# One group of V products per unit instead of two, with the softmax sums in its bank and the maxima turned by DMA

## The chip, the cores and the metric

The kernel runs on one core of a Trainium2 chip. The metric is the device time of one launch in microseconds; three runs are given as a median. Beside the runs stands one execution that the hardware profiler recorded.

## The reference

One encoder block is applied with shared weights to two requests of 2048 tokens (s = 0, 1). The part that matters here is the grouped-query attention: 8 query heads, 2 key/value heads of 64 channels, blocks of 128 queries.

```python
def one_block(qblk):
    s = jnp.einsum('bkgqd,bskd->bkgqs', qblk, k).astype(jnp.float32) * scale
    pr = jax.nn.softmax(s, axis=-1).astype(v.dtype)
    return jnp.einsum('bkgqs,bskd->bqkgd', pr, v)
...
a = _blocked_gqa(q, k, v) * jax.nn.silu(ga)
fo = _fourier_branch(f, w_fmix) * jax.nn.silu(gf)
h = h + jnp.concatenate([a, fo], axis=-1) @ w_out
gate = jax.nn.sigmoid(_rmsnorm(h, g_ple) @ w_ple_gate)
return h + (p @ w_ple) * gate
```

A block is 128 queries; those of a group's four heads (g) meet the 2048 keys of their key/value head (k). All inputs and outputs are float32.

## The kernel before

The program has three stages. First the input projection is computed for all tokens (line 451). Then attention runs, with the rest of the block, called filler here, between its pieces: the Fourier branch first (lines 1018, 1066, 1030), then the output projection and the gates token tile by token tile (lines 451, 1484, 1375 to 1538). What of the filler is left runs after attention.

Attention goes through 64 units `u`, each one request, one key/value head and one block of 128 queries, so four heads at once: 512 columns, head by head. A unit has eight steps `j`, one for each 256 keys. The loop at the end of `attention` counts steps as `g`, with u = g // 8 and j = g % 8. One step does this:

- `flush` runs what earlier steps deferred (divisions, stores).
- `scores`: TensorE multiplies queries and keys in fp16, in two row halves of 64 (shape 64*128, line 1147), into two PSUM banks. In step 0 a product of `kone` with `mr` first puts the negated row maxima there. ScalarE makes the exponentials `p` (line 1150), of fp32, one buffer `p32` a step. GpSimd adds them up over the steps into `acc` (lines 1153 and 1155) and after step 7 adds the two halves of `acc` (line 1157).
- `lead` runs 14 steps ahead: the score products for the maxima of a later unit (line 1174, into the only `ps_m` buffer) and their reduction on VectorE (line 1182). `negate` writes the negated maxima into `nm` in step 3 of the unit before.
- In step 4, `max_rows` turns `nm` with a TensorE product against the identity (line 1197, shape 128*128) and VectorE spreads it over the heads into `mr` (line 1199). `sums` makes the column sums of the unit before with a product of `acc` and ones (line 1243, shape 128*64), in the same bank, and `divide` takes their reciprocal there (line 1250) and multiplies (line 1251).
- In steps 0 and 4, after the rest, `pv` multiplies the exponentials of four steps with V in fp32 (line 1211, shape 128*64). Even and odd key chunks go to the two column halves, so that both halves of the result hold partial sums over keys of all four heads. `gather` adds them: ScalarE copies the crossed quarters (line 1227) and VectorE adds (line 1233).

After each step the loop yields a share, and `interleave` takes filler worth that share of the time that is left to spread. A step with `pv` yields 0. Filler is taken in whole slots. Every engine and the DMA queue of SyncE run their instructions one after the other: TensorE, ScalarE, VectorE and SyncE in the order in which the program writes them; GpSimd's order during attention is set by a scheduler.

Of the kernel before, what the change touches and what calls it, by code (L numbers as in the profile page):

```python
# [10 lines left out]
F32 = mybir.dt.float32  # L11
# [21 lines left out]
PVG = 4  # L33
# [7 lines left out]
P32 = 7  # L41
# [99 lines left out]
class Build:  # L141
# [963 lines left out]
    def attention(self, kvp):  # L1105
# [84 lines left out]
        def negate(u):  # L1190
            m = M4.pop(u)
            nc.scalar.activation(nm[:].rearrange("p (e c) -> p e c", e=2)[:, :, 0:4],
                                 m[:].unsqueeze(1).to_broadcast([128, 2, 4]), AF.Copy, scale=-1.0 / K_ONE)

        def max_rows(u, ps):

            nc.tensor.matmul(ps, nm[:], id16[:], start=True, stop=True)
            MR[u] = mr = kvp.tile([128, 4, 128], F16, name="mr", bufs=1)
            return lambda: nc.vector.tensor_tensor(out=mr[:], in0=ps.unsqueeze(1).to_broadcast([128, 4, 128]),
                                                   in1=own[:].unsqueeze(2).to_broadcast([128, 4, 128]), op=ALU.mult)  # L1200

        def pv(u, j0):
# [3 lines left out]
            o = O[u]  # L1206
            for j in range(j0, j0 + PVG):
                p = P.pop((u, j))
                for e in range(2):
                    c = 2 * j + e  # L1210
                    nc.tensor.matmul(o[64 * e:64 * e + 64, :], vt[s, kv, c // 8][:, c % 8, :], p[:, e, :],  # L1211
                                     start=(j == 0), stop=(j == 7))
            if j0 + PVG == 8:
# [3 lines left out]
                gather(u)  # L1217

        def gather(u):

            o = O.pop(u)
            tb = pool.tile([128, 2, 128], F32, name="tb", bufs=1)
            at = pool.tile([128, 2, 128], F32, name="at", bufs=2)
            AT[u] = at
            ov = o[:].rearrange("p (c e q) -> p e c q", e=2, q=128)
            for e in range(2):
                nc.scalar.activation(tb[64 * e:64 * e + 64], ov[64 - 64 * e:128 - 64 * e, e], AF.Copy,  # L1227
                                     scale=self.sc["a_scale"][64 - 64 * e:128 - 64 * e, :])

            def add():  # L1230
                for e in range(2):
                    sl = slice(64 * e, 64 * e + 64)
                    nc.vector.scalar_tensor_tensor(out=at[sl], in0=ov[sl, e], scalar=self.sc["a_scale"][sl, :],
                                                   in1=tb[sl], op0=ALU.mult, op1=ALU.add)

            self.defer(lambda: self.defer(add))

        def sums(u, ps):

            acc = ACC.pop(u)  # L1240
# [625 lines left out]
```

## Time and profile before

| | us |
|---|---|
| median of 3 runs (lowest, highest) | 2710.22 (2709.16, 2711.73) |
| span of the profiled execution | 2706.9 |
| median less that span | 3.3 |
| TensorE busy in it | 2623.5 |
| GpSimd busy in it | 1638.0 |
| VectorE busy in it | 1701.7 |
| ScalarE busy in it | 1215.2 |

The profiled execution has no time of its own beyond its span; the 3.3 us are what the runs have around it. In the profile PE is TensorE's matmuls, PEld its weight loads, DVE VectorE, ACT ScalarE, POOL GpSimd, SP SyncE. A shape such as 128*64 is the rows and columns of the array that an instruction uses. A matmul's duration includes its way through the array, and matmuls follow each other faster than that, so starts are compared.

### The profile page before, as it was taken

What the parts mean: (1) busy time and instruction counts of PE and PEld (TensorE: products, weight loads), DVE (VectorE), ACT (ScalarE), POOL (GpSimd) and SP (SyncE); (2) the same over time, 40 slices, a digit from 0 to 9 for tenths busy, and PEclk for the clock granted to TensorE, in tenths of its full rate; (3) what the DMA queues carried; (4) which work ended last, traced back from release to release, by engine and by line L of the source; (5) the groups of instructions that cost most, each with busy time, mean ns of one, the idle gap of its engine ahead of it and who ended that gap; (6) DMA issues with size and microseconds to landing.
All of it is one profiled execution on the core that took longest, in us unless ns stands there. A gap on an engine that the chain in (4) does not pass through costs nothing.

```text
span 2706.9 us, 46069 instructions
## 1 busy us (share of the span) xinstructions
PE 2623.5 (97%) x18112; PEld 1257.0 (46%) x18112; DVE 1701.7 (63%) x2478; ACT 1215.2 (45%) x2047; POOL 1638.0 (61%) x1395
## 2 busy tenths in 40 slices
PE   6899999999998998999999999999999999999998
PEld 3465565655555553444444444344444334444443
DVE  6756465565555785666676767665666666667634
ACT  4543243343224553554544555545545454454442
POOL 1233233242335896787777877777777777777760
PEclk9999999999999999999999999999999999999999
DMA  7467676586527663122222223322232222222222
GB/s 236 134 180 193 175 205 180 157 194 145 150 67 226 212 223 95 48 63 62 75 64 59 58 67 82 96 57 69 57 84 56 66 71 67 59 75 72 59 72 72
DMA packets 418553, 296.71 MB, mean 110 GB/s; under 512 B 259456, under 2 KB 360000, under 8 KB 418336
## 3 DMA queue, kind: packets, MB, share of 16 engines
q1 hardware_dynamic: 405424, 252.01, 35.4%
q0 software_dynamic: 12912, 41.77, 4.2%
q8 instruction: 141, 2.31, 0.3%
q14 instruction: 76, 0.62, 0.1%
HBM read 149.50 MB, written 86.51 MB: 87 GB/s over the span
## 4 chain that ended last, share of the span: by engine, by line
PE 89%; DVE 5%; issue 2%; ACT 1%; DMA 1%; POOL 0%; SPq 0%; DVEq 0%; ACTq 0%; POOLq 0%
PE ps_g L1484 22%; PE ps_x L451 17%; PE ps_o L1211 16%; PE ps_s L1147 13%; PE ps_f L451 7%; PE ps_g L451 7%; PE ps_m L1174 4%; PE ps_f L1243 1%; DVE a_mx L1182 1%; PE ps_g L1018 1%; PE ps_x L917 1%; DVE h L1524 1%; DVE w_mx L312 1%; PE ps_g L1066 0%; PE ps_f L1066 0%
## 5 line engine op out<-in xcount | busy, mean ns | idle before, releaser
L1155 POOL TENSOR_TENSOR acc<-acc,p 128x1024 f32<-128x1024 f32 x384 | 919.5, 2395 | 213.0 <-ACT p L1150 177.0
L1150 ACT ACTIVATE p<-ps_s,s_scale 128x512 f32<-128x512 f32 x1024 | 648.2, 684 | 649.7 <-PE ps_s L1147 624.9
L1182 DVE TENSOR_REDUCE a_mx<-ps_m 128x1 f32<-128x1024 f32 x498 | 609.1, 1223 | 521.3 <-PE ps_m L1174 513.7
L1484 PE MATMUL ps_g<-w_pg,hT 64*128 64x512 f16 x2784 | 493.9, 377 | 5.7 <-DMA hT<-h_hl 5.2
L1211 PE MATMUL ps_o<-p,v 128*64 128x512 f32 x2048 | 464.8, 596 | 0.0
L451 PEld LDWEIGHTS <-uc 128*128 128x128 f16 x3072 | 301.4, 98 | 311.4 <-issue 23.3
L1147 PE MATMUL ps_s<-q,k 64*128 64x512 f16 x3072 | 436.5, 378 | 5.2 <-ACT p L1150 5.2
L1484 PEld LDWEIGHTS <-hT 64*128 64x128 f16 x2784 | 205.2, 94 | 167.0 <-issue 21.4
L1147 PEld LDWEIGHTS <-k 64*128 64x128 f16 x3072 | 151.7, 94 | 249.5 <-issue 127.5
L1484 PE MATMUL ps_g<-w_wo,mh 64*128 64x512 f16 x1440 | 260.8, 377 | 2.8 <-DVE mh L1394 1.6
L1211 PEld LDWEIGHTS ps_o<-p,v 128*64 128x64 f32 x2048 | 141.4, 137 | 255.9 <-issue 246.7
L1484 PE MATMUL ps_g<-w_wo,mT 64*128 64x512 f16 x1440 | 257.7, 376 | 0.0
L1174 PE MATMUL ps_m<-k,q 64*128 64x512 f16 x996 | 202.9, 378 | 16.8 <-DVE a_mx L1182 12.5
L1153 POOL TENSOR_TENSOR acc<-p,p 128x1024 f32<-128x1024 f32 x64 | 150.8, 2356 | 72.8 <-ACT p L1150 72.2
L451 PEld LDWEIGHTS <-w_ga 128*128 128x128 f16 x1536 | 150.0, 99 | 47.2 <-issue 18.2
L934 POOL DMA_DIRECT2D gfd<-gt x32 | 19.6, 614 | 226.7 <-DVE gt L962 192.1
L1484 PEld LDWEIGHTS <-mh 64*128 64x128 f16 x1440 | 101.1, 94 | 91.8 <-issue 16.7
L1484 PEld LDWEIGHTS <-mT 64*128 64x128 f16 x1440 | 102.4, 94 | 83.6 <-issue 4.0
L1227 ACT ACTIVATE tb<-ps_o,a_scale 64x256 f32<-64x256 f32 x128 | 60.1, 469 | 165.8 <-PE ps_o L1211 165.0
L1250 DVE RECIPROCAL ps_f<-ps_f 128x256 f32<-128x256 f32 x59 | 103.6, 1756 | 16.3 <-PE ps_f L1243 16.3
L451 PE MATMUL ps_x<-uc,w_ga 128*128 128x256 f16 x960 | 108.1, 273 | 0.0
L952 POOL DMA_DIRECT2D agd<-gat x64 | 35.3, 553 | 118.4 <-DVE gat L962 113.2
(330 smaller groups left out, 3382.0 us busy)
## 6 DMA issues: line engine op xcount, KB each, us to landing
q<-qTd SPq DMA_DIRECT2D x256, 64.0 KB, 2.2
ag<-agd SPq DMA_DIRECT2D x64, 256.0 KB, 3.3
out<-h POOLq DMA_DIRECT2D x31, 512.0 KB, 3.0
x<-in_x_prompt SPq DMA_DIRECT2D x16, 512.0 KB, 4.7
gfd<-gt POOLq DMA_DIRECT2D x32, 256.0 KB, 2.6
gd<-ge POOLq DMA_DIRECT2D x32, 256.0 KB, 3.1
agd<-gat POOLq DMA_DIRECT2D x64, 128.0 KB, 2.7
w_st<-in_w_out SPq DMA_DIRECT2D x32, 256.0 KB, 3.8
```

What stands on the lines that cost most here:

```text
L451: self.nc.tensor.matmul(ps, lhs(ia, k), rhs(ib, k), start=(i == 0), stop=(i == 3 * ks - 1))
L952: nc.gpsimd.dma_start(self.agd[s][1, r * 128:(r + 1) * 128, c * n:(c + 1) * n], gt[:, :n])
L1147: nc.tensor.matmul(S[u][e][:], w[sl], q[sl].rearrange("p h q -> p (h q)"), start=j == i == 0, stop=i + 1 == len(todo), skip_group_check=True)
L1150: nc.scalar.activation(p[:, e, :], S[u][e][:], AF.Exp, scale=self.sc["s_scale"][:])
L1153: nc.gpsimd.tensor_tensor(out=ACC[u][:], in0=P[u, 0][:], in1=p[:], op=ALU.add)
L1155: nc.gpsimd.tensor_tensor(out=ACC[u][:], in0=ACC[u][:], in1=p[:], op=ALU.add)
L1174: nc.tensor.matmul(ps[c], Q[u][0][sl, h, :], kt[s, kv, half][sl, :, 0, :], start=True, stop=True)
L1182: nc.vector.reduce_max(MX[u][:, h, half, c:c + 1], x, axis=AX.X)
L1211: nc.tensor.matmul(o[64 * e:64 * e + 64, :], vt[s, kv, c // 8][:, c % 8, :], p[:, e, :], start=(j == 0), stop=(j == 7))
L1227: nc.scalar.activation(tb[64 * e:64 * e + 64], ov[64 - 64 * e:128 - 64 * e, e], AF.Copy, scale=self.sc["a_scale"][64 - 64 * e:128 - 64 * e ...
L1250: nc.vector.reciprocal(r, r)
L1484: nc.tensor.matmul(g[0][:], g[1](ia, k)[sl], g[2](ib, k)[sl], start=a, stop=z, skip_group_check=True)
```

## The change

`PVG` goes from 4 to 8: the products with V of a whole unit stand in one group, in step 0 of the next unit, and step 4 has none. The column halves no longer hold even and odd key chunks but two heads each: every chunk of V is loaded for both halves and multiplied with 256 columns in each, over all keys, so `gather` is not needed any more. The sums follow at once in the same group, into columns 256 to 511 of the same bank, and the division is deferred by one step: a reciprocal from PSUM to SBUF and one multiplication with the scale. The maxima are turned by a DMA transpose that SyncE issues in step 4; `nm` is four times as wide for it, and `mr` is written by the DMA. `p32` has ten buffers instead of seven, and the space for descriptors of GpSimd's DMAs is 4096 bytes a partition instead of 16384. Filler now has seven steps of a unit instead of six, by the expression with `PVG` in `run`, and deferred slow work runs three at a time after a group.

```diff
-PVG = 4
+PVG = 8
...
-P32 = 7
+P32 = 10
...
         def negate(u):
             m = M4.pop(u)
-            nc.scalar.activation(nm[:].rearrange("p (e c) -> p e c", e=2)[:, :, 0:4],
+            nc.scalar.activation(nm[:].rearrange("p h (e c) -> p e h c", e=2)[:, :, :, 0],
                                  m[:].unsqueeze(1).to_broadcast([128, 2, 4]), AF.Copy, scale=-1.0 / K_ONE)
 
-        def max_rows(u, ps):
-
-            nc.tensor.matmul(ps, nm[:], id16[:], start=True, stop=True)
+        def max_rows(u):
+
             MR[u] = mr = kvp.tile([128, 4, 128], F16, name="mr", bufs=1)
-            return lambda: nc.vector.tensor_tensor(out=mr[:], in0=ps.unsqueeze(1).to_broadcast([128, 4, 128]),
-                                                   in1=own[:].unsqueeze(2).to_broadcast([128, 4, 128]), op=ALU.mult)
+            nc.sync.dma_start_transpose(mr[:], nm[:].rearrange("p h c -> p (h c)"))
 
         def pv(u, j0):
...
-            o = O[u]
+            o, r = O[u][:, 0:256], O[u][:, 256:512]
             for j in range(j0, j0 + PVG):
-                p = P.pop((u, j))
+                p = P.pop((u, j))[:].rearrange("p e (c f q) -> p e f c q", f=2, q=128)
                 for e in range(2):
                     c = 2 * j + e
-                    nc.tensor.matmul(o[64 * e:64 * e + 64, :], vt[s, kv, c // 8][:, c % 8, :], p[:, e, :],
-                                     start=(j == 0), stop=(j == 7))
+                    for f in range(2):
+                        nc.tensor.matmul(o[64 * f:64 * f + 64], vt[s, kv, c // 8][:, c % 8, :], p[:, e, f],
+                                         start=(c == 0), stop=(c == 15))
...
-                gather(u)
-
-        def gather(u):
...
-        def sums(u, ps):
...
+                av = ACC.pop(u)[:, 0, :].rearrange("p (c f q) -> p f c q", f=2, q=128)
+                for f in range(2):
+                    nc.tensor.matmul(r[64 * f:64 * f + 64], self.ones[:], av[:, f], start=True, stop=True)
+                self.defer(lambda: divide(u))
+
+        def divide(u):
+
+            s, kv, t = units[u]
+            at = pool.tile([128, 2, 128], F32, name="at", bufs=2)
             o = O.pop(u)
...
-            nc.vector.reciprocal(r, r)
-            nc.vector.tensor_tensor(out=x, in0=x, in1=r, op=ALU.mult)
+            nc.vector.reciprocal(x, o[:, 256:512])
+            nc.vector.scalar_tensor_tensor(out=x, in0=o[:, 0:256], scalar=self.sc["a_scale"][:], in1=x,
+                                           op0=ALU.mult, op1=ALU.mult)
...
             if j == 4:
-                ps = self.bank()
                 if u + 1 < n:
-                    turned = max_rows(u + 1, ps[:, 256:384])
-                if u > 0:
-                    sums(u - 1, ps[:, 0:256])
-                    divide(u - 1, ps[:, 0:256])
-                if u + 1 < n:
-                    turned()
+                    max_rows(u + 1)
             heavy = (g - 1) % PVG == PVG - 1 and 0 <= g - 1 < 8 * n
             if heavy:
-                self.run_slow(1 if j else 2)
+                self.run_slow(3)
                 pv((g - 1) // 8, (g - 1) % 8 - PVG + 1)
...
-    nc = bacc.Bacc("TRN2", target_bir_lowering=False, num_devices=1)
+    nc = bacc.Bacc("TRN2", target_bir_lowering=False, num_devices=1, dynamic_dma_scratch_size=4096)
```

In the changed kernel the lines shift: the products with V are L1210, the sums L1218, the transpose L1198, the division L1227 and L1228, and what was L1375, L1484 and L1526 is L1343, L1452 and L1494.

TensorE before, in step 4 of a unit around 1500 us: the maxima of a later unit, the turning of `nm`, the sums of the unit before, four steps' products with V, and the next step's scores (a row x2 is one product for each column half).

```order
L1174 MATMUL ps_m<-k_7155,q_15561 128x512
L1197 LDWEIGHTS nm
L1197 MATMUL ps_f<-id_7187,nm 128x128
L1243 MATMUL ps_f<-acc,ones 64x256 x2
L1211 MATMUL ps_o<-p_15567,v_7161 64x512 x2
L1211 MATMUL ps_o<-p_15600,v_7161 64x512 x2
L1211 MATMUL ps_o<-p_15637,v_7161 64x512 x2
L1211 MATMUL ps_o<-p_15672,v_7161 64x512 x2
L1147 LDWEIGHTS k_7158
```

TensorE after, in step 0 of the next unit at about the same place: the maxima, the one group with eight steps' products and the sums, and then filler.

```order
L1174 MATMUL ps_m<-k_7171,q_15434 128x512
L1210 MATMUL ps_o<-p_15440,v_7177 64x256 x4
L1210 MATMUL ps_o<-p_15495,v_7177 64x256 x4
L1210 MATMUL ps_o<-p_15535,v_7177 64x256 x4
L1210 MATMUL ps_o<-p_15563,v_7177 64x256 x4
L1210 MATMUL ps_o<-p_15624,v_7179 64x256 x4
L1210 MATMUL ps_o<-p_15658,v_7179 64x256 x4
L1210 MATMUL ps_o<-p_15692,v_7179 64x256 x4
L1210 MATMUL ps_o<-p_15708,v_7179 64x256 x4
L1218 MATMUL ps_o<-acc,ones 64x256 x2
L1452 LDWEIGHTS mh
```

The product with `nm` is gone from TensorE, the sums moved from step 4 to the end of step 0, behind L1210, and step 4's maxima are followed by filler.

GpSimd before, in the 50th unit: its seven additions, the addition of the two halves, and a filler addition L1375 that needs loaded data.

```order
L1153 TENSOR_TENSOR acc<-p_23038,p_23113 128x1024
L1155 TENSOR_TENSOR acc<-acc,p_23150 128x1024
L1155 TENSOR_TENSOR acc<-acc,p_23185 128x1024
L1155 TENSOR_TENSOR acc<-acc,p_23221 128x1024
L1155 TENSOR_TENSOR acc<-acc,p_23253 128x1024
L1375 TENSOR_TENSOR ag<-ag 128x512
L1155 TENSOR_TENSOR acc<-acc,p_23293 128x1024
L1155 TENSOR_TENSOR acc<-acc,p_23328 128x1024
L1157 TENSOR_TENSOR acc<-acc 128x512
L1526 DMA out<-h 128x1024
```

GpSimd after, in the same unit:

```order
L1153 TENSOR_TENSOR acc<-p_23503,p_23560 128x1024
L1343 TENSOR_TENSOR ag<-ag 128x512
L1155 TENSOR_TENSOR acc<-acc,p_23596 128x1024
L1155 TENSOR_TENSOR acc<-acc,p_23634 128x1024
L1155 TENSOR_TENSOR acc<-acc,p_23671 128x1024
L1155 TENSOR_TENSOR acc<-acc,p_23700 128x1024
L1155 TENSOR_TENSOR acc<-acc,p_23740 128x1024
L1155 TENSOR_TENSOR acc<-acc,p_23768 128x1024
L1157 TENSOR_TENSOR acc<-acc 128x512
L1494 DMA out<-h 128x1024
```

The filler addition moved from behind the fifth addition to behind the first.

VectorE after, at a unit's edge (before, the division stood in step 4 as L1250, L1251 and L1199):

```order
L1362 SCALAR_TENSOR_TENSOR mh<-ag,mix_s,mh 128x1024
L1227 RECIPROCAL at<-ps_o 128x256
L1228 SCALAR_TENSOR_TENSOR at<-ps_o,a_scale,at 128x256
L1182 TENSOR_REDUCE a_mx<-ps_m 128x1
L1187 TENSOR_REDUCE a_m_14922<-a_mx 128x4
```

The division stands directly ahead of step 1's reduction of maxima (L1182), which completes a unit's maxima (L1187).

More of the change, by code (lines that the diff above doesn't have):

```diff
@@ L1216, in pv @@
                         del vt[s, kv, b]
-                gather(u)
-        def gather(u):
-            o = O.pop(u)
[L1222 to L1236, printed above, removed]
-        def sums(u, ps):
-            acc = ACC.pop(u)
-            av = acc[:, 0, :].rearrange("p (c e q) -> p e c q", e=2, q=128)
-            for e in range(2):
-                nc.tensor.matmul(ps[64 * e:64 * e + 64], self.ones[:], av[:, e], start=True, stop=True)
-        def divide(u, r):
-            s, kv, t = units[u]
-            at = AT.pop(u)
+                av = ACC.pop(u)[:, 0, :].rearrange("p (c f q) -> p f c q", f=2, q=128)
[5 more added lines that the diff above has]
+            at = pool.tile([128, 2, 128], F32, name="at", bufs=2)
+            o = O.pop(u)
             x = at[:].rearrange("p c q -> p (c q)")
-            nc.vector.reciprocal(r, r)
-            nc.vector.tensor_tensor(out=x, in0=x, in1=r, op=ALU.mult)
+            nc.vector.reciprocal(x, o[:, 256:512])
+            nc.vector.scalar_tensor_tensor(out=x, in0=o[:, 0:256], scalar=self.sc["a_scale"][:], in1=x,
+                                           op0=ALU.mult, op1=ALU.mult)
             def store():
@@ L1262, in attention @@
             load_q(kv)
-        id16 = kvp.tile([128, 128], F16, name="id16", bufs=1)
-        nc.gpsimd.tensor_copy(id16[:], self.ident[:])
-        nm = kvp.tile([128, 128], F16, name="nm", bufs=1)
+        nm = kvp.tile([128, 4, 128], F16, name="nm", bufs=1)
         nc.gpsimd.memset(nm[:], 0.0)
@@ L1268, in attention @@
         nc.gpsimd.memset(kone[:], K_ONE)
-        own = kvp.tile([128, 4], F32, name="own", bufs=1)
-        nc.gpsimd.tensor_tensor(out=own[:], in0=self.ident[:, 0:4], in1=self.ident[:, 64:68], op=ALU.add)
         def lead(g):
@@ L1284, in leads @@
                 if g == -2:
-                    max_rows(0, self.bank()[:, 0:128])()
+                    max_rows(0)
         self.ahead = leads()
```

## Prediction

> **What bounds the kernel now.** I read the page's totals first, then the chain that ended last, then busy time by stage.
>
> ```profile
> span 2706.9 us, 46069 instructions
> PE 2623.5 (97%) x18112; PEld 1257.0 (46%) x18112; DVE 1701.7 (63%) x2478; ACT 1215.2 (45%) x2047; POOL 1638.0 (61%) x1395
> PE 89%; DVE 5%; issue 2%; ACT 1%; DMA 1%; POOL 0%; SPq 0%; DVEq 0%; ACTq 0%; POOLq 0%
> ...
> 871.00:1011.00 140.00, 135.77 (x962) 78.07 (x963) 107.94 (x143) 82.89 (x137) 123.96 (x72) 1.00 0.68 216
> ...
> 1100.00:1700.00 600.00, 592.96 (x4414) 249.36 (x4412) 406.66 (x422) 305.00 (x509) 462.34 (x370) 1.00 0.25 66
> ...
> 2300.00:2628.00 328.00, 327.36 (x2469) 137.79 (x2467) 200.17 (x203) 163.14 (x270) 247.72 (x213) 1.00 0.24 66
> ```
>
> The columns of a stretch are PE, PEld, DVE, ACT, POOL, granted clock, DMA share. In the two long stretches PE is busy all but 1% of the time at full clock, and the chain is 89% PE. So a microsecond taken from PE's stream is a microsecond of the kernel, and work taken from DVE or ACT is worth nothing by itself. POOL is the second engine to watch: 77% in the long stretch (462.34 of 600), 89% in the Fourier stretch (123.96 of 140). The sum is made against this execution's 2706.9 us span; the median of the runs is 2710.22, 3.3 us above it, and I carry those 3.3 us over unchanged. What this kernel's measurement can tell from no change is about 0.2%, 5.4 us.
>
> **PE, the term that pays.** The two groups of one unit, the one of step 4 and the one of step 0, as PE ran them:
>
> ```profile
> 1496.47 0.40 PE L1174 MATMUL ps_m<-k,q 64*128 64x512 f16 x2
> 1496.80 0.23 PE L1197 MATMUL ps_f<-id,nm 128*128 128x128 f16 x1
> 1496.96 0.65 PE L1243 MATMUL ps_f<-acc,ones 128*64 128x256 f32 x4
> 1497.44 3.60 PE L1211 MATMUL ps_o<-p,v 128*64 128x512 f32 x16
> 1500.98 0.82 PE L1147 MATMUL ps_s<-q,k 64*128 64x512 f16 x6
> ...
> 1509.06 0.39 PE L1147 MATMUL ps_s<-mr,kone 64*128 64x512 f16 x2
> 1509.28 0.81 PE L1147 MATMUL ps_s<-q,k 64*128 64x512 f16 x6
> 1509.93 0.38 PE L1174 MATMUL ps_m<-k,q 64*128 64x512 f16 x2
> 1510.24 3.65 PE L1211 MATMUL ps_o<-p,v 128*64 128x512 f32 x16
> 1513.83 0.82 PE L1147 MATMUL ps_s<-q,k 64*128 64x512 f16 x6
> 1514.48 0.38 PE L1174 MATMUL ps_m<-k,q 64*128 64x512 f16 x2
> 1514.70 0.38 PE L1484 MATMUL ps_g<-w_wo,mh 64*128 64x512 f16 x1
> ```
>
> Starts are what counts, since ends overlap. The weight loads beside the first group give the rhythm inside it:
>
> ```profile
> 1496.96 0.20 PEld L1243 LDWEIGHTS ps_f<-acc,ones 128*64 128x64 f32 x4
> 1497.23 0.36 PEld L1211 LDWEIGHTS ps_o<-p,v 128*64 128x64 f32 x4
> 1497.88 0.14 PEld L1211 LDWEIGHTS ps_o<-p,v 128*64 128x64 f32 x2 [0.29 <-issue]
> 1498.30 0.14 PEld L1211 LDWEIGHTS ps_o<-p,v 128*64 128x64 f32 x2 [0.29 <-issue]
> 1498.73 0.14 PEld L1211 LDWEIGHTS ps_o<-p,v 128*64 128x64 f32 x2 [0.29 <-issue]
> ```
>
> Each fp32 product shows as two instructions, one pass each, and the two column halves run side by side. A pair of 512-column passes takes 0.43 us (1498.30 to 1498.73), and eight of them make 3.43 us.
>
> Step 4 costs 1500.98 - 1496.47 = 4.51 us from the maxima to the next scores; step 0 costs 1513.83 - 1509.93 = 3.90 us. An ordinary step goes from its maxima to the next work in 0.22 us (1514.48 to 1514.70). So one visit to this shape costs 3.90 - 3.43 - 0.22 = 0.25 us beyond its columns, and step 4, with a third shape ahead of it for L1197, costs 4.51 - 3.43 - 0.22 - 0.43 = 0.43 us beyond its columns and the sums'.
>
> The changed unit has one visit: 32 pair-passes of 256 columns for V, then two for the sums. What does such a pass cost? Below stands half of 0.43, 0.215 us; above stands the sums group as it is, 1496.96 to 1497.44, 0.48 us for two, or 0.24 us each. The second number holds the exposed first load of a visit (step 0's first pass starts at 1510.24 and the group needs 0.05 us more than step 4's for the same columns: 1513.83 - 1510.24 is 3.59 against 1500.98 - 1497.44 = 3.54). Without those 0.05 the two take 0.43, so I use 0.216. The ends of the bound are 34 x 0.215 = 7.31 and 34 x 0.24 = 8.16 us.
>
> After: 0.25 + 34 x 0.216 + 0.22 = 7.81 us, and step 4 becomes ordinary, 0.22. Saved: 4.51 + 3.90 - 7.81 - 0.22 = 0.38 us a unit, 64 units, **24.3 us**. With 0.24 a pass it would be a loss of 0.44 us a unit, 28 us. Filler now stands in seven steps instead of six; counting shape changes in the new order, it enters and leaves its 128x128 shape 13 times more, at about 0.1 us each: **1.3 us** back. PE's net is **-23.0 us**.
>
> By the Trainium skill's TensorEngine Tiling (Array Packing), Instruction Overhead, a matmul has about 60 cycles of overhead; as an addition to each of the 16 extra pair-passes that is an estimated 25 ns each, 26 us in all, and the gain is gone. By its TensorE: Matmul & The Clock Gate, Part 3, a weight load overlaps a matmul in flight only where the row group differs. Both halves use all rows here, so by it the 16 extra loads of 0.14 us would show, 2.2 us a unit; the trace disagrees, since 0.14 us loads already fit inside a 0.43 us rhythm of bare columns.
>
> **POOL, the term that takes.** The sums need the last addition of L1157. Today PE asks for it four steps into the next unit; now at the end of step 0's group. Two units, POOL at their edge; the next unit's first scores start at 1509.06 and 2229.55:
>
> ```profile
> 1502.96 9.66 POOL L1155 TENSOR_TENSOR acc<-acc,p 128x1024 f32<-128x1024 f32 x4
> 1512.70 2.13 POOL L1157 TENSOR_TENSOR acc<-acc 128x512 f32<-128x512 f32 x1
> ...
> 2229.55 0.39 PE L1147 MATMUL ps_s<-mr,kone 64*128 64x512 f16 x2
> ...
> 2229.60 1.27 POOL L1375 TENSOR_TENSOR ag<-ag 128x512 f32<-128x512 f32 x1 [4.15 <-DVE a_mx L1182]
> 2230.83 5.67 POOL L1155 TENSOR_TENSOR acc<-acc,p 128x1024 f32<-128x1024 f32 x2
> 2236.57 2.12 POOL L1157 TENSOR_TENSOR acc<-acc 128x512 f32<-128x512 f32 x1
> ```
>
> The new sums would start 1510.24 - 1509.06 + 0.05 + 32 x 0.216 = 8.1 us after those scores. In the first unit POOL is done 5.8 us after them, 2.3 us early; in the second 9.1 us after, 1.0 us late. Everything PE has queued stands behind that wait. How often?
>
> ```profile
> L1155 POOL TENSOR_TENSOR acc<-acc,p 128x1024 f32<-128x1024 f32 x384 | 919.5, 2395 | 213.0 <-ACT p L1150 177.0
> L1153 POOL TENSOR_TENSOR acc<-p,p 128x1024 f32<-128x1024 f32 x64 | 150.8, 2356 | 72.8 <-ACT p L1150 72.2
> L1157 POOL TENSOR_TENSOR acc<-acc 128x512 f32<-128x512 f32 x64 | 94.4, 1475 | 4.9
> POOL ag L1375 <- DMA ag<-agd: 54.7, 23, 7.2
> PE ps_m L1174 <- DVE a_mx L1182: 12.5, 15, 1.7
> L1150 ACT ACTIVATE p<-ps_s,s_scale 128x512 f32<-128x512 f32 x1024 | 648.2, 684 | 649.7 <-PE ps_s L1147 624.9
> L1251 DVE TENSOR_TENSOR at<-at,ps_f 128x256 f32<-128x256 f32 x59 | 24.8, 421 | 2.0
> L1227 ACT ACTIVATE tb<-ps_o,a_scale 64x256 f32<-64x256 f32 x128 | 60.1, 469 | 165.8 <-PE ps_o L1211 165.0
> L1250 DVE RECIPROCAL ps_f<-ps_f 128x256 f32<-128x256 f32 x59 | 103.6, 1756 | 16.3 <-PE ps_f L1243 16.3
> DMA to landing us min/median/max: 3.0/3.1/5.8
> ```
>
> (The last row is of hT's 64 transposes.) The additions are (919.5 + 150.8 + 94.4) / 64 = 18.2 us a unit. A unit now takes (2229.55 - 1509.06) / 26 = 27.7 us, 26 units lying between those two scores; in the Fourier stretch five units take the 140 us, 28.0 each. So with filler POOL works 0.771 x 27.7 = 21.3 us a unit in the long stretch and 0.885 x 28.0 = 24.8 in the Fourier stretch. After the change it gets its first addition only when the group's sums (0.43), step 1's scores (0.65), two exponentials (1.37) and, by estimate, 1 us of filler are through, 3.5 us, so it has 27.7 - 0.4 - 3.5 = 23.8 us before the next sums, or 24.1. In the long stretch 2.5 us are to spare on average; in the Fourier stretch 0.7 are missing in each of five units, which with its unevenness I take for **6 us**. In the long stretch POOL stands 23 times at L1375 for a landing, 2.4 us on average, just what is spare. The new order puts L1375 earlier in its unit, which helps, but seven additions now follow each other with no PE group among them, so that less is caught up. I take half of those 23 units as late by 1 us: **11 us**. The bounds are nothing, as the first unit shows, and the second unit's 1.0 us in each of 57 units with the 6 before, 63 us; I stay near the first end, since the averages leave time.
>
> **The other edits.** The division (1.76 us and, like L1251, 0.42) now stands on DVE ahead of step 1's maximum, and PE's next maxima wait for that reduction. From the sums' end that is 2.2 us of division and, like any reduction, about 1.2 us, 3.4 us, against two score groups, one maxima and two filler slots on PE, about 1.5 + 2.6. It is hidden where the slots are full, and DVE loses L1199, the multiply and two half-height passes in exchange; L1174 waits 12.5 us in all now. I take **0**, with bounds of -5 and +10. ACT loses L1227, 60 us of work that nothing on the chain waits for: 0. The transpose of the maxima is issued at step 4, behind `negate` of step 3, and is needed four steps, some 10 us, later; landing takes 3.1, at most 5.8 us. SP stands there until ACT has written `nm`, and what queues behind are loads and stores of later steps: 0, bounds 0 and 5. The store of `at` leaves three steps earlier than now, which nobody waits for. Ten buffers hold a unit's eight and two more, so no exponential waits for the later release: 0. For POOL's smaller descriptor space no row shows a wait: 0, bounds 0 and 5.
>
> **Sum.** -23.0 + 6 + 11 = -6 us. Some of PE's small waits of today, the 12.5 us at L1174 among them, will fall together with waits for POOL, worth by estimate another 2 us: 2706.9 - 8 = 2699 of span, and with the 3.3 us outside it **2702 us**.
>
> **Rivals.** With W for PE's waits at the sums, the time is 2710.2 - 25 + W; my forecast is W from 10 to 20, its own range 2695 to 2705.
> - POOL is in time nearly everywhere, W under 10, about 5: 2690. For it: L1375 moves earlier. Against: the second unit above. Chance 0.17.
> - POOL takes the whole gain, W from 20 to 30: 2710, no change. For it: 0.8 us in each of some 30 units is enough. Against: 2.5 us spare on average. Chance 0.24.
> - Slower by POOL: PE stands at L1218 for L1157 by more than 0.48 us a unit on average, W over 30, the point from which it decides. At 0.75 us, W is 48: 2733. For it: POOL's additions are pressed together at 77% load, and the second unit is late already. Against: the first is 2.3 us early. Chance 0.19.
> - A 256-column pass costs the upper 0.24 us: 28 us lost instead of 24.3 gained, with the same waits 2754. Against: the 0.05 us of the first load explain that bound. Chance 0.02.
> - Weight loads show, 16 more a unit at 0.14 us: 64 x 2.24 = 143 us more, 2845. Against: the rhythm above. Chance 0.02.
> - The transposed maxima come late to each unit's first scores, by 1 us: 2702 + 64 = 2766; it would take landings beyond 10 us. Chance 0.01.
>
> **Numbers.** The forecast has chance 0.35. Faster by over 0.2% (under 2704.8) is it and the first rival, 0.52; within 0.2% is the second, 0.24; slower is the rest, 0.24. The range is 2687 to 2728: the low end is PE's net without a wait, the high end holds about half of the slower rival and leaves out some 0.15 above.
>
> **What would show it.** L1210's weight loads should start 0.216 us apart, and one unit should show one L1210 group of about 7 us. L1218 should wait for POOL's last addition, 6 us in total before 1011 us and some 11 later; under 5 or over 25 in total decides between the rivals. L1174's waits should stay near 12 us, and the first scores should never wait for `mr`. A rhythm above 0.22 us, or a wait ahead of the step-1 maxima, would make the prediction wrong.

## The result and the profile after

The changed kernel is slower: 2771.8 us (median of four runs, 2769.4 to 2779.2) against 2711.0 us for the kernel before in the same job, a ratio of 1.0228 with an interval of 1.0213 to 1.0243. That is 61 us more, where 8 us less was forecast; the rival that named PE standing at the sums for POOL had been given 2733 us.

From the page of the changed kernel, its span, busy times and chain:

```profile
span 2767.6 us, 49738 instructions
...
PE 2634.8 (95%) x20096; PEld 1428.1 (52%) x20096; DVE 1648.8 (60%) x2286; ACT 1153.6 (42%) x1919; POOL 1660.6 (60%) x1393
...
PE 67%; POOL 16%; DVE 7%; issue 4%; DMA 3%; ACT 3%; SPq 1%; POOLq 0%; DVEq 0%; ACTq 0%
```

Two of the stretches shown of before, with the same columns (PE, PEld, DVE, ACT, POOL, granted clock, DMA share):

```profile
871.00:1011.00 140.00, 136.46 (x1106) 91.64 (x1104) 97.45 (x126) 78.14 (x126) 122.55 (x71) 0.99 0.76 231
1100.00:1700.00 600.00, 568.59 (x4838) 289.66 (x4836) 366.28 (x337) 267.59 (x438) 448.07 (x344) 0.99 0.27 65
```

PE's share of the chain fell from 89% to 67%, POOL's rose from 0 to 16%, DVE's from 5 to 7%. In the stretch from 1100 to 1700 us PE has holes of 31 us where it had 7. The Fourier stretch, where I had seen POOL fullest, is nearly as before.

Two successive units on PE, the first in time, the second not:

```profile
1332.70 0.40 PE L1174 MATMUL ps_m<-k,q 64*128 64x512 f16 x2
1333.02 7.13 PE L1210 MATMUL ps_o<-p,v 128*64 128x256 f32 x64
1339.98 0.60 PE L1218 MATMUL ps_o<-acc,ones 128*64 128x256 f32 x4
1340.51 0.82 PE L1147 MATMUL ps_s<-q,k 64*128 64x512 f16 x6
...
1359.12 0.38 PE L1174 MATMUL ps_m<-k,q 64*128 64x512 f16 x2
1359.43 7.13 PE L1210 MATMUL ps_o<-p,v 128*64 128x256 f32 x64
1370.26 1.04 PE L1218 MATMUL ps_o<-acc,ones 128*64 128x256 f32 x4 [3.69 <-POOL acc L1157]
1371.23 1.46 PE L1147 MATMUL ps_s<-q,k 64*128 64x512 f16 x6
1372.48 0.63 PE L1174 MATMUL ps_m<-k,q 64*128 64x512 f16 x2
```

In the first unit the way from the maxima to the next scores is 1340.51 - 1332.70 = 7.81 us, exactly the figure of the prediction's sum. In the second the sums stand 3.69 us for POOL, and what follows then takes nearly double (1.46 us for the scores instead of 0.82). Why POOL was late there:

```profile
1342.78 2.35 POOL L1153 TENSOR_TENSOR acc<-p,p 128x1024 f32<-128x1024 f32 x1 [1.39 <-ACT p L1150]
1351.40 1.27 POOL L1343 TENSOR_TENSOR ag<-ag 128x512 f32<-128x512 f32 x1 [6.27 <-DMA ag<-agd]
1352.63 16.24 POOL L1155 TENSOR_TENSOR acc<-acc,p 128x1024 f32<-128x1024 f32 x6
1368.94 1.26 POOL L1157 TENSOR_TENSOR acc<-acc 128x512 f32<-128x512 f32 x1
```

It stood 6.27 us for the filler's landing behind its first addition, and then had six additions and L1157 to make up without a gap. The stretches around that stop (the granted clock stands behind the five engines):

```profile
1370.50:1374.00 3.50, 3.50 (x18) 0.99 (x16) 2.63 (x3) 1.28 (x3) 0.28 (x1) 0.53 0.38 150
1374.00:1377.50 3.50, 3.50 (x36) 1.56 (x34) 2.13 (x3) 2.29 (x3) 2.94 (x2) 1.00 0.21 44
```

PE ran at 0.53 of its clock for the 3.5 us behind its stop, and ran 18 matmuls there against 36 in the next 3.5 us.

There is a second kind of stop, two steps behind the sums. In a unit around 1767 us, PE from step 1's scores to step 2's maxima, and VectorE beside it:

```profile
1767.32 0.82 PE L1147 MATMUL ps_s<-q,k 64*128 64x512 f16 x6
1767.98 0.38 PE L1174 MATMUL ps_m<-k,q 64*128 64x512 f16 x2
1768.19 1.46 PE L1452 MATMUL ps_g<-w_pg,hT 64*128 64x512 f16 x12
1769.49 0.87 PE L1147 MATMUL ps_s<-q,k 64*128 64x512 f16 x6
1770.90 0.39 PE L1174 MATMUL ps_m<-k,q 64*128 64x512 f16 x2 [0.54 <-DVE a_mx L1182]
...
1767.43 1.76 DVE L1227 RECIPROCAL at<-ps_o 128x256 f32<-128x256 f32 x1 [4.00 <-PE ps_o L1218]
1769.23 0.48 DVE L1228 SCALAR_TENSOR_TENSOR at<-ps_o,a_scale,at 128x256 f32<-128x256 f32 x1
1769.63 1.22 DVE L1182 TENSOR_REDUCE a_mx<-ps_m 128x1 f32<-128x1024 f32 x1
```

The division holds back step 1's reduction, which ends at 1769.63 + 1.22 = 1770.85. PE's step 1 is short here, with one slot of 12 filler products. So PE has its scores of step 2 behind it early, and the next maxima wait for the only `ps_m` buffer: they come 1.41 us after the scores, 0.75 us later than in step 1 (0.66).

The waits that answer to those of before (total, times, longest):

```profile
POOL ag L1343 <- DMA ag<-agd: 83.7, 22, 7.8
...
PEld ps_o L1218 <- POOL acc L1157: 52.7, 33, 4.1
...
PE ps_o L1218 <- POOL acc L1157: 38.0, 28, 3.7
...
PE ps_m L1174 <- DVE a_mx L1182: 16.1, 31, 1.2
...
PE ps_s L1147 <- ACT p L1150: 11.7, 46, 0.6
```

PE and its weight loads wait for the same thing, so their two rows overlap. To get one number for each place I also took the time from one matmul's start to the next in attention, less the normal spacing (0.216 us, for fp32 with 512 columns 0.43), wherever it exceeds that by 0.12 us, and call it a stop. Matmuls in a stretch with half the granted clock exceed it too, so the clock's loss is partly inside these sums. All stops are 49 us before and 125 us after. Before L1218 stand 43 us, in 30 units; before the maxima of step 2 stand 21 us (8 before the change), of which 4 are, in both kernels, one wait for loaded queries in the first unit. The others go with the length of step 1, taken from its scores to those of step 2: of 29 units in which it takes up to 2.45 us, 23 have such a stop; of 34 in which it takes longer, one.

### The profile page after: what moved, and what is told of

Its sections match the earlier page's. It is cut to its first block, busy times and chain, and to the rows that moved or that the text cites. A ratio compares the mean times of both kernels' runs of the same rounds, so it can differ in the third digit from the quotient of the medians.

```text
span 2767.6 us, 49738 instructions
## 1 busy us (share of the span) xinstructions
PE 2634.8 (95%) x20096; PEld 1428.1 (52%) x20096; DVE 1648.8 (60%) x2286; ACT 1153.6 (42%) x1919; POOL 1660.6 (60%) x1393
## 4 chain that ended last, share of the span: by engine, by line
PE 67%; POOL 16%; DVE 7%; issue 4%; DMA 3%; ACT 3%; SPq 1%; POOLq 0%; DVEq 0%; ACTq 0%
PE ps_x L451 16%; PE ps_g L1452 15%; POOL acc L1155 11%; PE ps_o L1210 8%; PE ps_s L1147 8%; PE ps_g L451 7%; PE ps_f L451 6%; PE ps_m L1174 2%; ACT p L1150 2%; POOL acc L1157 2%; DMA ag<-agd 2%; DVE a_mx L1182 1%; DVE at L1227 1%; PE ps_o L1218 1%; PE ps_x L917 1%
## 5 line engine op out<-in xcount | busy, mean ns | idle before, releaser
L1155 POOL TENSOR_TENSOR acc<-acc,p 128x1024 f32<-128x1024 f32 x384 | 935.1, 2435 | 95.0 <-ACT p L1150 55.3
L1182 DVE TENSOR_REDUCE a_mx<-ps_m 128x1 f32<-128x1024 f32 x498 | 608.3, 1221 | 396.4 <-PE ps_m L1174 387.1
L1452 PE MATMUL ps_g<-w_pg,hT 64*128 64x512 f16 x2784 | 502.9, 377 | 8.6 <-DMA hT<-h_hl 5.1
L1210 PE MATMUL ps_o<-p,v 128*64 128x256 f32 x4096 | 456.9, 381 | 0.0
L1147 PE MATMUL ps_s<-q,k 64*128 64x512 f16 x3072 | 447.7, 380 | 8.4 <-ACT p L1150 8.3
L1210 PEld LDWEIGHTS ps_o<-p,v 128*64 128x64 f32 x4096 | 288.8, 137 | 166.5 <-issue 28.1
L1452 PEld LDWEIGHTS <-hT 64*128 64x128 f16 x2784 | 207.5, 94 | 166.4 <-issue 18.6
L1452 PE MATMUL ps_g<-w_wo,mh 64*128 64x512 f16 x1440 | 265.2, 380 | 1.2 <-DVE seen L1418 1.2
L1147 PEld LDWEIGHTS <-k 64*128 64x128 f16 x3072 | 163.1, 94 | 197.6 <-issue 70.9
L1452 PE MATMUL ps_g<-w_wo,mT 64*128 64x512 f16 x1440 | 260.6, 379 | 0.0
L1227 DVE RECIPROCAL at<-ps_o 128x256 f32<-128x256 f32 x64 | 112.4, 1756 | 246.5 <-PE ps_o L1218 246.5
L1452 PEld LDWEIGHTS <-mh 64*128 64x128 f16 x1440 | 103.7, 95 | 87.8 <-issue 20.7
L1452 PEld LDWEIGHTS <-mT 64*128 64x128 f16 x1440 | 106.2, 95 | 73.1 <-issue 5.3
L1174 PEld LDWEIGHTS <-q 64*128 64x128 f16 x1024 | 67.8, 95 | 95.0 <-issue 39.9
L1157 POOL TENSOR_TENSOR acc<-acc 128x512 f32<-128x512 f32 x64 | 103.0, 1610 | 4.9
L451 PE MATMUL ps_x<-w_f,uc 128*128 128x512 f16 x480 | 105.9, 379 | 0.0
```

The costliest lines, as they stand in the source:

```text
L451: self.nc.tensor.matmul(ps, lhs(ia, k), rhs(ib, k), start=(i == 0), stop=(i == 3 * ks - 1))
L1147: nc.tensor.matmul(S[u][e][:], w[sl], q[sl].rearrange("p h q -> p (h q)"), start=j == i == 0, stop=i + 1 == len(todo), skip_group_check=True)
L1155: nc.gpsimd.tensor_tensor(out=ACC[u][:], in0=ACC[u][:], in1=p[:], op=ALU.add)
L1157: nc.gpsimd.tensor_tensor(out=ACC[u][:, 0, :], in0=ACC[u][:, 0, :], in1=ACC[u][:, 1, :], op=ALU.add)
L1174: nc.tensor.matmul(ps[c], Q[u][0][sl, h, :], kt[s, kv, half][sl, :, 0, :], start=True, stop=True)
L1182: nc.vector.reduce_max(MX[u][:, h, half, c:c + 1], x, axis=AX.X)
```

## The experiments

Times are medians; the kernel before had 2710.3 to 2711.8 us in the jobs concerned, so differences are taken from the changed kernel's 2771.8 us or from the 2711 us of the kernel before.

**Is it the sums?** Two runs that relieve the place where PE stood, and one that gives POOL a step more.

```diff
...
+            if j == 2 and u > 0:
+                sums(u - 1)      # the products of L1218, then divide deferred as before
...
```

> The changed kernel with the sums (and with them the division behind) taken out of the group and put after the maxima of step 2, two steps later, in a visit of their own. Theory A (the loss is PE standing at the sums for GpSimd's last addition, 43 us in the changed kernel's trace, and what these stops entail, the half-clock stretches behind them): the wait at the sums falls below 4 us, the half-clock stretches during attention fall to two or three, and the additional visit costs 0.25 to 0.43 us a unit, 16 to 27 us: 2772 - 43 - 20 + 20 = about 2729 us, 2715 to 2742. Theory B (seven microseconds of products in one piece starve ScalarE, GpSimd and VectorE wherever the sums stand, and the wait only changes its place): the waits in front of scores and maxima grow by what the sums lose, and with the visit it is 2775 to 2795 us.

Measured 2742.1 us. The stop at the sums is gone, 30 us come back and the extra visit takes its part; but theory A wanted 13 us more. The stops before maxima did not go: 19.5 us of them moved from step 2 to step 4, again two steps behind the sums.

```diff
-  lambda: TM.update({t: self.defer(lambda: nc.gpsimd.tensor_tensor(
+  lambda: TM.update({t: self.defer(lambda: nc.vector.tensor_tensor(
       out=ag[:, 0], in0=ag[:, 0], in1=ag[:, 2], op=ALU.mult))}),
```

> The changed kernel with one edit: the filler's multiplication of loaded attention rows (ag, line 1343, 32 of 1.3 us) on VectorE instead of GpSimd, so that GpSimd neither does it nor stands for its landing (83.7 us in 22 waits in the changed kernel's trace). Theory A1 (GpSimd is late at the sums because it stood for these landings): the wait at the sums falls from 43 to about 15 us, the time to 2735 us, 2722 to 2748. Theory A2 (GpSimd is late because its seven additions of 18 us a unit get their first operand only after the group, landings or not): it stays above 30 us, and the time above 2755 us. VectorE may stand for the landings instead and hold up the maxima; that would show as waits for a_mx beyond the 27 us of the changed kernel.

Measured 2741.9 us; the stop before the sums fell from 43 to 9 us. So these 32 instructions make most of POOL's lateness, and the seven additions behind each other make little by themselves. The edit takes two things off POOL at once, the standing for landings (A1) and the multiplication's own 1.27 us; the changed kernel's trace speaks for the standing. All 16 units with a stop over 0.9 us at the sums have such an instruction, and in 13 of them, with 32 of the 43 us, POOL had stood 1.8 to 6.3 us ahead of it. VectorE pays for the edit: the stops before maxima rise from 28 to 39 us.

```diff
-            heavy = (g - 1) % PVG == PVG - 1 and 0 <= g - 1 < 8 * n
+            heavy = (g - 2) % PVG == PVG - 1 and 0 <= g - 2 < 8 * n
...
-                pv((g - 1) // 8, (g - 1) % 8 - PVG + 1)
+                pv((g - 2) // 8, (g - 2) % 8 - PVG + 1)
...
```

> The changed kernel with the whole group (products with V and sums) one step later, in step 1 of the next unit; the other steps that follow the group (embedded products) move along, and one scale of the second request is computed in a fixed step. No visit is added, GpSimd has one step (about 2.6 us) more for its last addition, and the first addition of the next unit can run beside the group. Theory A: the wait at the sums falls from 43 to under 5 us, half-clock stretches to two or three, 2772 - 43 - 20 = about 2707 us, 2692 to 2718; with all of the knock-on waits gone too it ends below the kernel before, near 2695. Theory B: the stop stays in another place, 2755 us or more.

Measured 2763.1 us, where theory A said 2707. POOL's wait went as expected, and another one came up:

```profile
PE ps_m L1174 <- DVE a_mx L1182: 29.5, 40, 3.0
...
PE ps_s L1147 <- ACT p L1150: 25.8, 79, 0.6
...
PE ps_o L1218 <- POOL acc L1157: 4.0, 3, 2.1
```

The stops at the sums are 5 us, those at the maxima two steps behind them 32 us, and those before scores 43 us (24 in the changed kernel). Theory A, one cause, had fallen. In all three runs the second stop follows the sums at a distance of two steps; the division stands on VectorE in the step between, ahead of its reduction. That made theory C: two waits.

**Each wait alone, and both.** Three ablations. The first leaves out the reciprocal, so that the products are only scaled; the second divides by the sums of the unit before, which are long ready; the third does both.

```diff
-            nc.vector.reciprocal(x, o[:, 256:512])
-            nc.vector.scalar_tensor_tensor(out=x, in0=o[:, 0:256], scalar=self.sc["a_scale"][:], in1=x,
-                                           op0=ALU.mult, op1=ALU.mult)
+            nc.vector.tensor_scalar(out=x, in0=o[:, 0:256], scalar1=self.sc["a_scale"][:], scalar2=None, op0=ALU.mult)
```

> The changed kernel without the division on VectorE: the reciprocal is left out and the products are only scaled (one instruction of about 0.4 us instead of two of 2.2 us together). It isolates the division. Theory C: the waits at the maxima of step 2 fall from 20.9 to below 6 us, the wait at the sums stays at 35 to 48 us: 2772 - 17 - a few = 2750 us, 2744 to 2757. Theory B (the group starves the maxima by itself): the waits at step 2 stay above 15 us, and the time above 2763 us.

```diff
-                av = ACC.pop(u)[:, 0, :].rearrange(...)
+                av = (ACC.pop(u - 1) if u else ACC[0])[:, 0, :].rearrange(...)
```

> The changed kernel with the sums taken of the `acc` of the unit before (so a unit is divided by its predecessor's sums), which has been ready for a whole unit; every instruction stays, GpSimd's additions too, and only PE's wait for the last addition goes. Theory C: the wait at the sums is 0 to 2 us, the half-clock stretches that followed these waits go too (10 us), the waits at step 2's maxima stay near 21 us or grow a little: 2772 - 43 - 10 = 2719 us, 2711 to 2728. Theory B: the waits come back in front of scores and maxima, 2745 us or more.

> Both of these edits together in the changed kernel: no reciprocal, and the sums of the unit before. Theory C: the two effects add up, 2772 - 53 - 20 = about 2699 us, 2690 to 2707: what then lies below 2710.5 us is the gain of the one group and of the turned maxima. If the gains of the change itself were mis-sized, it ends at 2712 us or more although both waits are gone; if the two waits hide each other, the saving here is below 0.8 times or above 1.2 times the sum of the savings of the single edits.

Measured 2749.8 us without the reciprocal, 2727.8 us with the sums of the unit before, 2694.9 us with both (0.9942 of the kernel before, interval 0.9928 to 0.9955). The waits in these three, in that order:

```profile
PE ps_o L1218 <- POOL acc L1157: 39.6, 26, 4.0
...
PE ps_m L1174 <- DVE a_mx L1182: 1.1, 4, 0.5
```

```profile
PE ps_m L1174 <- DVE a_mx L1182: 22.7, 36, 2.7
...
PEld ps_o L1218 <- POOL acc L1157: 0.5, 1, 0.5
```

```profile
PE ps_m L1174 <- DVE a_mx L1182: 2.0, 5, 0.9
...
PEld ps_o L1218 <- POOL acc L1157: 0.5, 1, 0.5
```

Each edit takes away its own wait and leaves the other. The division is worth 22 us, POOL 44 us, both together 77 us. 77 is 1.17 times 22 + 44, so the two hide each other a little: with POOL's wait gone, the stops at step 2's maxima grew from 21 to 29 us. All that the change lost is in these two: without them it would be 16 us faster than the kernel before. Theory B, that seven microseconds in one piece starve whatever follows, is out.

**Place or amount of the division?** Issued behind step 1's reduction instead of ahead of it:

```diff
-                self.defer(lambda: divide(u))
...
+            if j == 1 and u > 0:
+                divide(u - 1)     # behind lead(g), so behind this step's reduction
```

> The changed kernel with the division issued behind step 1's reduction of the maxima on VectorE instead of ahead of it; nothing is left out. If the division's place makes the second wait, the waits at step 2's maxima fall from 20.9 to below 6 us, waits at step 3's maxima rise by less than 6, the wait at the sums stays near 43: 2772 - 18 = 2754 us, 2747 to 2760. If its amount makes it (VectorE has no 2.2 us to spare in two steps without a group), the wait moves to step 3 and the time stays at 2765 us or more.

Measured 2775.8 us. The stops at step 2's maxima fell to 5 us and came back at step 3's (22 us), and filler in step 2 stops 20 us (4 in the changed kernel). So it is the amount, not the place: a short step of 2.2 us, like the one above, leaves VectorE 1 us beside its reduction of 1.2, and the division takes 2.2.

**One part of the change alone**, on the kernel before: the maxima turned by DMA, both groups and the sums as they were.

```diff
...
-                ps = self.bank()
                 if u + 1 < n:
-                    turned = max_rows(u + 1, ps[:, 256:384])
+                    max_rows(u + 1)      # nc.sync.dma_start_transpose, as in the changed kernel
+                ps = self.bank()
                 if u > 0:
                     sums(u - 1, ps[:, 0:256])
                     divide(u - 1, ps[:, 0:256])
-                if u + 1 < n:
-                    turned()
```

> The kernel before with one part of the change alone: the maxima turned by the DMA transpose into mr (wider nm, no product with the identity, no VectorE spreading), with a descriptor space of 8192 bytes to make room. The sums stay in step 4 and both groups of four stay. By the prediction's working, the third shape ahead of step 4's group costs 0.18 us more than one visit: 64 x 0.18 = 11.5 us saved, 2710.2 - 11.5 = 2699 us, 2695 to 2704. Rival 1: the third shape cost nothing that PE did not lose anyway, 2710 us. Rival 2: the transposes delay other loads on SyncE or the first scores wait for mr: 2713 us or more.

Measured 2702.0 us, 0.9968 (0.9956 to 0.998) of the kernel before, so 5 to 12 us less. Step 4 on PE:

```profile
1494.98 0.40 PE L1174 MATMUL ps_m<-k,q 64*128 64x512 f16 x2
1495.31 0.65 PE L1241 MATMUL ps_f<-acc,ones 128*64 128x256 f32 x4
1495.79 3.60 PE L1209 MATMUL ps_o<-p,v 128*64 128x512 f32 x16
1499.33 0.82 PE L1147 MATMUL ps_s<-q,k 64*128 64x512 f16 x6
```

It takes 1499.33 - 1494.98 = 4.35 us instead of 4.51, 0.16 us less in each of 64 units, 10 us. (This run has 8192 bytes of descriptor space, the changed kernel 4096.) No rival to this part came true.

**The whole computation without the two waits.** ScalarE copies the scaled products out of `ps_o`; the sums stand in a bank of their own at the head of the next unit's group, a whole unit after POOL began, and the division runs beside that group, as it did before the change.

```diff
+                nc.scalar.activation(at[:].rearrange("p c q -> p (c q)"), O.pop(u)[:, 0:256], AF.Copy,
+                                     scale=self.sc["a_scale"][:])
...
                 self.run_slow(3)
+                if u > 1:
+                    sums(u - 2)       # and reciprocal, multiplication, store deferred
                 pv((g - 1) // 8, (g - 1) % 8 - PVG + 1)
```

> The changed kernel with the sums a whole unit later: ScalarE copies the scaled products out of ps_o into `at`, and the sums of that unit stand, in a bank of their own, at the head of the next unit's group, with the division behind them on VectorE beside the 7 us of that group (embedded products in steps 1, 2 and 6 instead of 1, 2 and 7). One group a unit as before, no visit added. Theory C (two waits of the changed kernel, not one: PE at the sums for GpSimd, 43 us, and PE at the maxima two steps after the sums, because the division of 2.2 us stands ahead of the reduction on VectorE with no group of products beside it, 21 us; each run so far showed the second, two steps behind the sums: 19.5 us with the sums in step 2, 31.8 us with the group in step 1): both go, with some 10 us of half-clock stretches: 2772 - 43 - 21 - 10 = about 2697 us, 2688 to 2706. If the division is not the cause of the second wait, 2712 us or more. If one group of 7 us a unit cannot be fed whatever follows it, 2720 us or more.

Measured 2784.3 us: wrong by 87 us, though hardly anything is left of either wait. Two of PE's waits:

```profile
PE ps_s L1147 <- ACT p L1150: 48.3, 149, 1.3
...
PE ps_m L1174 <- DVE a_mx L1182: 1.1, 4, 0.5
```

Scores follow scores there with little filler between, and PE waits for the exponentials: the stops before scores are 87 us, 81 of them in steps 5 to 7 and 0, most after 2000 us. The rows `at` are stored seven steps later, the filler's tile needs them, and its deferred slow work runs only ahead of a group; so when filler catches up with attention it runs out (theory D). Three runs on that reading started from this version; two changed when the slow work runs, and the middle one, on top of the first, when the filler's multiplication is issued:

```diff
+            if j in (1, 2, 3, 4, 5, 6, 7) and self.slow:
+                self.run_slow(1)
...
-                self.run_slow(3)
+                self.run_slow(1)
```

> The kernel of the run with the sums at the head of the next group (2784 us), with one edit: the filler's deferred slow work (three pieces of about 1.1 us on VectorE for a token tile) is run one at a time in any step, not three at a time ahead of the group only. Theory D (that run was slow because `at` was stored seven steps later, so that the filler's next tile got its slow work only at the following group, and in steps 4 to 7 there was no filler left: PE stood 82 us at scores for ScalarE): by the program's order the stops of the filler fall from 99 to 31 (39 in the changed kernel), the waits in front of scores from 82 to about 20 us, and the time from 2784 to about 2700 us, 2692 to 2712. Rival E (stores or sums a unit late cost by themselves, or ScalarE's copy does): above 2740 us. Slow work beside a step without products may hold up the maxima: up to 15 us more.

```diff
-PAD = 6
+PAD = 0
```

> The same, and the six empty places between the filler's loads and its multiplication on GpSimd taken out, so that GpSimd may stand for the landing instead of the multiplication being issued later. GpSimd has a whole unit of slack before its sums here. If theory D holds and slack remains, GpSimd's waits for landings rise and nothing else does: within 4 us of the run beside it. If GpSimd's standing reaches PE again, 10 us or more above it.

```diff
+            if j in (4,) and self.slow:
+                self.run_slow(1)      # and run_slow(3) ahead of the group
```

> The run with the sums at the head of the next group, with one piece of slow work in step 4 beside the three ahead of the group: a smaller dose of the same cure; the filler's stops fall from 99 to 42. Theory D: 2700 to 2725 us, above the run with slow work in any step by some 5 to 20 us. Rival E: above 2750 us.

Measured 2792.2, 2748.8 and 2728.7 us. The first missed by 92 us: PE no longer waits so long for exponentials, but now for what the slow work makes, and for maxima.

```profile
PE ps_g L1458 <- DVE mh L1368: 32.6, 9, 4.6
...
PE ps_m L1174 <- DVE a_mx L1182: 30.9, 36, 2.9
```

By my reading of the program, which no run tests alone, the filler's order counts slow work as done one flush earlier, which 7 us of products beside it make true and an ordinary step does not. In the second the filler's multiplication is issued earlier and 43 us of that go, though I had expected no effect; its DVE `mh` wait is 8.8 us. The third, with one piece in step 4, is best, 4 us above its range, and still loses; I had expected it to be slower than the first. A cleaner test was to leave the slow work alone and let filler lag a little, in the version of 2784.3 us and, as a control, in the changed kernel:

```diff
-FILL = 765.0
+FILL = 758.0
```

> The version with the sums at the head of the next unit's group (2784 us), with one number changed: 758 instead of 765 us of filler are spread over attention, so that the filler's tiles lag a little more behind the units whose rows they need. By the program's order the filler's stops fall from 99 to 35, without any slow work in other steps. Theory D with C: the waits in front of scores fall from 82 to about 20 us, and with both waits of the changed kernel gone the time is near that of the run with both ablations, 2697 us, 2688 to 2712. Rival E (sums a unit late, or ScalarE's copy, cost by themselves): above 2750 us.

> Control: the changed kernel with 758 instead of 765 us of filler and nothing else. By theory C its waits at the sums and at the maxima of step 2 stay: 2765 to 2780 us. Below 2750 us the amount of filler would be a cause of its own.

Measured 2719.7 and 2797.3 us, 8 and 17 us above their ranges. The control is 25 us slower than the changed kernel: 7 us less filler leave more work for the end (from the last scores to the span's end 111 us instead of 91, and 112 in the other run), which I had not thought of. Against its control the version with both waits gone saves 78 us, the 77 us of the ablations. The last pair, again on the version of 2784.3 us, spreads the filler otherwise and leaves its amount; the second of them also computes one scale of the second request in a fixed step:

```diff
-RATE = 1.15
+RATE = 1.3      (the other run: 1.2)
```

> The version with the sums at the head of the next unit's group (2784 us, 765 us of filler), with one number changed: the later half of the steps gets 1.3 instead of 1.15 shares of filler, so that the filler's tiles lag behind the units in the middle and catch up only at the end. By the program's order the filler's stops fall from 99 to 31, and as much filler as in the changed kernel (759.5 us; 758.0 there) is done in attention. Theory C: no wait at the sums, the waits at the maxima near 10 us, no more work left at the end: about 2697 us, 2689 to 2706, below the kernel before and near the kernel before with turned maxima alone (2702 us). If the distribution itself costs (shorter steps first, longer ones later), 2710 us or more.

> The same with 1.2 shares (and one scale of the second request in a fixed step), where the filler's stops are 40 by the program's order. Theory C: 2700 us, 2690 to 2710; like the other version within 8 us, since neither runs out of filler.

Measured 2700.1 us (0.9951, interval 0.9937 to 0.9965) and 2697.4 us (0.9948, 0.9934 to 0.9961): both faster than the kernel before, with nothing left out, and 72 to 74 us faster than the changed kernel. The last one's span and chain, and its middle stretch:

```profile
span 2695.6 us, 49936 instructions
...
PE 88%; DVE 4%; ACT 3%; issue 2%; DMA 1%; SPq 0%; POOL 0%; DVEq 0%; ACTq 0%; POOLq 0%
```

```profile
1100.00:1700.00 600.00, 593.45 (x5174) 315.08 (x5172) 385.82 (x358) 296.43 (x491) 480.14 (x374) 1.00 0.29 72
```

PE's holes in the stretch are 6.5 us, as before the change, POOL is out of the chain although it is busier in that stretch (480 us instead of 448), and the clock is full. Against this run the version of 2784.3 us has 66 us more of stops (119 against 53) and 17 us more behind the last scores (109 against 92). The first of the pair, with 1.3 for RATE and nothing else changed, takes 84 us off. So the loss of that version lay in how the filler was spread.

## Why the prediction was wrong, step by step

- *PE, -23.0 us*: right in kind, a little large in size. The group came as drawn, 7.81 us from maxima to scores. With both waits ablated the gain over the kernel before is 16 us; its stops are 3 us more than before's, so PE's own part is some 19 us. The turned maxima alone bring 8.5 of it (11.5 by the prediction's step). The 32 pair-passes with V took 1339.98 - 1333.02 = 6.96 us, 0.2175 each. So neither weight loads nor the upper bound of 0.24 us show, nor an addition of 25 ns to each of the extra passes; both of those rivals are out. No run shows the 0.1 us for a change of shape by itself.
- *W = 6 in the Fourier stretch + 11 later*: the failed term. Before 1011 us it is 1 us, not 6; later it is 42 us, not 11; 30 units wait, up to 3.9 us each. The step that failed reads "2.5 us to spare on average" and then takes half of 23 units as late by 1 us. It took a mean wait of 2.4 us, and it took it from the old order. Set one by one against the 2.5 us, the waits for landings in that row that lie inside attention (22; the longest, 7.2 us, stands behind it) exceed it by 13 us in all, and by 22 with the waits at L1375 that the profile puts down to other engines. So single waits instead of the mean would have raised the 11 us by at most as much again. The larger part is that the waits grew: in the changed kernel those at L1343 inside attention exceed 2.5 us in 19 units, by 35 us in all, and 13 of these units stop at the sums, for 30 of the 43 us.
- *"The new order puts L1375 earlier in its unit, which helps"*: it did not, and the forecast rests on it. The instruction is early on POOL, but its data are not; POOL stands for landings 83.7 us instead of 54.7, and with that instruction on VectorE the stop fell from 43 to 9 us. Why the landings are that late stays open.
- *The division 0, bounds -5 and +10*: wrong, 22 us by the ablation. VectorE's side of the sum was right: 3.4 us from the end of the sums to the end of the reduction (1767.43 to 1770.85), and in 21 of the 24 units that stop nothing of the filler stands on VectorE in between. PE's side failed: it took two filler slots, 2.6 us, as standing beside it, and a step with one slot of 1.3 us leaves 2.8 us against 3.4. "Hidden where the slots are full" was there, but not a count of the steps in which they are not. Before the change 3.4 us of products with V stood beside the division.
- *Small waits fall together, -2*: the other way. Behind long stops the clock is granted at half: in attention such stretches are 37.5 us in the changed kernel's trace, 13.7 before, 17.1 with both waits ablated. At half speed that loses about (37.5 - 13.7) / 2 = 12 us, an estimate from the clock rows; no run changed the clock alone, and it is inside the 77 us. Only the 20.5 us of it behind the stops at the sums are clearly theirs: in the run with the sums of the unit before they are gone, yet that trace has 34.1 us, 27.3 of them before 1100 us (17.0 in the changed kernel).
- *Transposed maxima, ACT, p32, descriptor space at 0*: right. The weight loads waited 0.4 us, once, for `mr`; the run with turned maxima alone, on 8192 bytes of descriptor space, shows no new wait.
- *The rivals*: "slower by POOL" was the mechanism, with a chance of 0.19 and W of 48, close to the 43 measured. It priced one wait and 2733 us; the other 39 us are the division, the clock, their overlap and a gain on PE some 4 us smaller.

## What to carry to other kernels

When a consumer is moved earlier, set each single wait in the producer's queue against the spare time of a unit, not the mean wait; and above all ask what the new order does to those waits, since here they grew. How late the producer ends in the old order is not enough: in the trace of before only 11 of 63 last additions would have missed the new due time of 8.1 us, by 7 us in all. When work is moved off a stage, look at what else that stage had covered: the group in step 4 hid a division of 2.2 us that nobody waited for until the group was gone. The shortest step beside it, and not the full one, decides whether it stays hidden. Two waits of that kind each look like the whole cause until each is ablated alone and both together.

## What the hardware showed that I had not expected

A stop of PE of 2 to 4 us can be followed by 3.4 us at half the granted clock: 0.53 in the 3.5 us behind the stop of 3.69 us, and six such stretches in attention that the kernel before has not, each beginning from 0.4 us before to 1.3 us after the end of a stop at the sums of 2.0 to 3.9 us. Stops of 3.3 and 3.5 us in two other units, and of 2.3 in a third, had none behind them. The six begin 17, 17, 17, 57 and 253 times 3.413 us apart, so the granted clock changed on a fixed grid here; my reading is that a stop's place on that grid decides whether it is hit. So a long stop at the sums costs more than its length. The Trainium skill's TensorE: Matmul & The Clock Gate, Part 1, puts half rate behind at least one idle window of about 3.4 us, on a window that runs freely; the trace agrees in the length of a stretch and in that not every stop is hit, but stops shorter than that window were enough here.
